# First wave of a one-layer encoder: four adaLN column tiles computed on TensorE, with ten more landing buffers

## Chip, core and metric

The kernel runs on one core of a Trainium2 chip. The metric is device time in microseconds (us) for one execution of the whole program. A core has five engines that run side by side, each with its own instruction queue in program order: TensorE (PE in the profile, with its weight loads shown as PEld), VectorE (DVE), ScalarE (ACT), GpSimd (POOL) and SyncE (SP), which here issues the DMA transfers between HBM and the on-chip memory. Products go to PSUM, which has eight banks of 128 x 512 floats.

## What is computed

One layer of an encoder over 2048 tokens of width 1024, everything in float32. A conditioning vector c gives six vectors of 1024 (shift, scale and gate for each of two sublayers); the first sublayer is windowed attention, the second a SwiGLU network. Cut to the part that matters here:

```python
c_act = silu(c)
mod = c_act @ ada_w + ada_b                    # 1024 -> 6 * 1024
sh1, sc1, g1, sh2, sc2, g2 = split(mod, 6)
h = rmsnorm(x, mix_norm_pre) * (1 + sc1) + sh1
qkv = h @ w_qkv                                # 1024 -> 1536
x = x + g1 * rmsnorm(attention(qkv) @ w_o, mix_norm_post)
h = rmsnorm(x, ffn_norm_pre) * (1 + sc2) + sh2
x = x + g2 * rmsnorm(swiglu(h), ffn_norm_post)
```

So the first product of the layer, `h @ w_qkv`, can start only when the norm of x and the first tiles of sh1 and sc1 exist.

## The kernel before

**Layout.** Activations are held transposed: width on the 128 partitions (KT = 8 tiles k of 128 rows), tokens along the free dimension, in four chunks of CH = 512 tokens. A float32 product is made of three products of a shorter format (`three`, line 839): each operand is split into a high part `hi` and a rest `lo` (`split`, line 845: ScalarE copies to `hi`, a second engine subtracts to get `lo`), and hi\*hi, hi\*lo and lo\*hi are added up in PSUM.

**The first wave** is the part that the change touches (lines 966 to 982). It works on chunk 0 and on seven of the twelve 128-column tiles of w_qkv (WAVE = 7), and keeps seven PSUM banks open while k runs from 0 to 7. Before the loop, `squares0` (line 877) squares the eight x tiles on ScalarE and adds them in pairs on VectorE, and `norm` (line 887, `rstd_of` at line 810) sums over the partitions by a product with a tile of ones (plain float32 operands, which the profile shows as two MATMULs for each product), then takes Ln and Exp on ScalarE and one correction step: Square on ScalarE, three operations on VectorE. Then, for each k:

- two tiles of ada_w, one for the scale and one for the shift (128 x 1024 floats each), are loaded (`ada_load`, line 945) and each is multiplied with silu(c) and summed along its rows by one VectorE instruction (`ada_reduce`, line 950). For this, `cb` holds silu(c) copied to all 128 partitions.
- `coef` = (1 + scale) \* gain, a 128 x 1 operation on VectorE;
- `w_piece(k, 0)` (line 955) loads 896 columns of w_qkv and splits them, the subtraction being recorded for GpSimd;
- `Chunk.h` (line 891): x \* r on VectorE, then scale and shift on ScalarE, then a cast to `hi` on ScalarE, then `lo` on VectorE;
- 21 products of 128 x 512 on TensorE (7 tiles, 3 products each).

After the loop come the rests of the w_qkv columns (`w_piece(k, 1)`, 640 columns, into the pool w2), the five other tiles of chunk 0, then chunk 1 with all twelve tiles, then attention with chunks 2 and 3 as filler, the output projection and the feed-forward part.

**Buffers.** All loads of ada_w and w_qkv land in one pool `raws` with five buffers of 128 x 1024 floats (line 933); pool w2 (line 932) holds the split rests of w_qkv, 40 KB in each partition.

**Order.** The program does not fix the order of instructions. All operations are first recorded (`Recorder`, line 136); a planner (`schedule`, line 683) then simulates them with a cost for each (`cost`, line 246), chooses the order on every engine, the buffer of every tile and, for subtractions recorded for GpSimd, whether GpSimd or VectorE does them (`others`, line 225), and repeats this 18 times with priorities taken from the run before. DMAs are in the same plan, all on SP's queue. So a local edit gives a new plan for the whole program. All instructions are emitted from one line, 748, so the profile is read by tile names: `ada` (tiles of ada_w), `wqkv` (raw weights), `w` (split weights), `x`, `hi`, `lo`, `nsq` (squares), `nr` and `nta` (the norm), `cb`, `mod`, `coef`, and `bank` for PSUM.

Of the kernel before, what the change touches and what calls it, by code (L numbers as in the profile page):

```python
# [20 lines left out]
P = 128  # L21
S = 2048
D = 1024
# [31 lines left out]

OBUFS = 6

HOLD = 6

PARTS = ((2, 3, 3, 3), (3, 3, 3, 2))  # L60
# [24 lines left out]
class Buf:  # L85


    def __init__(self, rec, name, shape, dtype, pool, tag):
        self.name, self.shape, self.dtype, self.pool, self.tag = name, list(shape), dtype, pool, tag
        self.row = int(np.prod(shape[1:]))  # L90
        self.unit = 1 if self.row <= P else DH
        self.log, self.ops, self.slot, self.real = [], set(), None, None


class Tag:
# [40 lines left out]
class Recorder:  # L136
# [41 lines left out]
    def record(self, eng, fn, args, kw):  # L178
        op = Op()
        op.i, op.eng, op.fn, op.args, op.kw, op.ins = len(self.ops), eng, fn, args, kw, None  # L180
        aps = [(j, x) for j, x in list(enumerate(args)) + list(kw.items()) if isinstance(x, bass.AP)]
        out = {0}
        if fn == "custom":
            out = {1}
        elif fn == "tensor_tensor_reduce":
            out = {0, 7}
        elif fn == "activation" and "accum_out" in kw:
            out = {0, "accum_out"}
        op.writes = [self.region(x) for j, x in aps if j in out]
        op.reads = [self.region(x) for j, x in aps if j not in out]  # L190
        op.tiles = []
        if fn == "matmul" and not kw.get("start"):
            op.reads.append(op.writes[0])
        elif fn == "matmul":
            op.writes = [(op.writes[0][0], (3, (1 << P) - 1))]
        outs, ins = [x for j, x in aps if j in out], [x for j, x in aps if j not in out]
        op.forms, op.calls, op.stamp = {}, {}, 0
        for op.eng, op.fn, op.args, op.kw in (*self.others(eng, fn, args, kw, ins), (eng, fn, args, kw)):
            self.cost(op, outs, ins)
            op.forms[op.eng] = op.occ, op.lat, op.port, op.table  # L200
            op.calls[op.eng] = op.fn, op.args, op.kw
        op.eng_first = eng
        op.pred = {}
        for w, items in ((False, op.reads), (True, op.writes)):
            for b, m in items:
                for q, qw, qm in b.log:
                    if (w or qw) and q is not op and qm[0] & m[0] and qm[1] & m[1]:
                        op.pred[q] = max(op.pred.get(q, 0), self.gap(q, op))
        for w, items in ((False, op.reads), (True, op.writes)):
            for b, m in items:  # L210
                if w:
                    b.log = [e for e in b.log if not (e[2][0] | m[0] == m[0] and e[2][1] | m[1] == m[1]) or e[0] is op]
                b.log.append((op, w, m))
                if b.tag is not None and op not in b.ops:
                    if not b.ops:
                        b.tag.order.append(b)
                    b.ops.add(op)
                    op.tiles.append(b)
        op.succ = []
        for q in op.pred:  # L220
            q.succ.append(op)
        self.ops.append(op)
        return op
# [22 lines left out]
    def cost(self, op, outs, ins):  # L246
# [12 lines left out]
        elif eng == "pe":  # L259
            if fn == "transpose":  # L260
                op.occ, op.lat = 108, 330
            elif outs[0].dtype == F32 and ins[0].dtype == F32:
                op.occ, op.lat = 860 * n // CH, 1060 * n // CH
            else:
                op.occ = n * 0.4167 + 13.5
                op.lat = op.occ + 162
# [487 lines left out]
    return ap.bitcast(F32)  # L754


def row(ap, n):

    return bass.AP(tensor=ap.tensor, offset=ap.offset, ap=[[0, P], [1, n]])
# [3 lines left out]
def encoder_layer(ctx, tc, a):  # L763
# [34 lines left out]
    mod = const.tile([P, 80], F32, name="mod")  # L798
    adab = constr.tile([P, 48], F32, name="adab")
    gains = constr.tile([P, 4, KT], F32, name="gains")  # L800
    nsink = const.tile([P, HEADS], F32, name="nsink")
    ones = const.tile([P, P], F32R, name="ones")
    ident = const.tile([P, P], F32, name="ident")
# [52 lines left out]
    class Chunk:  # L856
# [20 lines left out]
        def squares0(self):  # L877

            sq = [hs.tile([P, CH], F32, tag=("hi", "lo")[k % 2], name=f"nsq0_{k}") for k in range(KT)]
            for k in range(KT):  # L880
                act.activation(sq[k], self.xt[k], AF.Square)
                if k % 2:
                    dve.tensor_tensor(sq[k - 1], sq[k - 1], sq[k], ALU.add)
            dve.tensor_tensor(sq[6], sq[4], sq[6], ALU.add)
            self.acc = [sq[0], sq[2], sq[6]]

        def norm(self, psp, ptag):
            r = nrm.tile([P, CH], F32, tag="nr", name=f"nr{self.c}")
            self.r = rstd_of(rot(nrm, "nsq", 2), psp, ptag, self.acc, f"a{self.c}", r)
# [39 lines left out]


    with ExitStack() as pa:
        w2 = open_pool(pa, "w2", side="right")
        raws = open_pool(pa, "raws", 5, side="right")
        w1 = open_pool(pa, "w1", side="right")
        psA = open_pool(pa, "psA", 8, space=PSUM)

        cb = nrm.tile([P, D], F32, name="cb")
        sp.dma_start(cb, row(a["c"], D))
        ch0 = Chunk(0)
        sp.dma_start(adab, a["ada_b"])  # L940
        sp.dma_start(gains, a["gains"])
        act.activation(cb, cb, AF.Silu)
        sp.dma_start(cb_d, cb)

# [5 lines left out]
        def ada_reduce(t, w):  # L950
            dve.tensor_tensor_reduce(w, w, cb, 1.0, adab[:, t:t + 1], ALU.mult, ALU.add, mod[:, t:t + 1])

        wres = {}

        def w_piece(k, i):
            pl, lo_c, n = ((w1, 0, C1), (w2, C1, C2))[i]
# [24 lines left out]
        for k in range(KT):  # L981
# [847 lines left out]
```

## Time and profile before

| what | value |
|---|---|
| median of three runs | 2037.0 us (2036.87 to 2037.06) |
| the profiled execution's own time | 2036.67 us |
| span of its instructions | 2034.9 us |
| mean granted TensorE clock | 0.995 of full speed |
| TensorE busy | 1991.0 us (98%) |
| VectorE busy | 1703.6 us (84%) |
| ScalarE busy | 1069.9 us (53%) |
| GpSimd busy | 554.4 us (27%) |
| HBM traffic | 278.52 MB read, 134.77 MB written |

In the lines of the profile, a timeline row gives the start, the length, the engine, the source line, the operation, `out<-in`, the shape and how many were merged into the row; in brackets stands how long the engine had been idle before and what released it. A row of the windows view gives, for a stretch of time, the busy time of each engine and its number of instructions, the granted clock (PEclk), the busy share of the DMA engines and their rate. A group row ends with the busy time in us and the mean of one in ns. Matmuls are pipelined: a row of eight that lasts 1.98 us holds eight that start 0.227 us apart.

### The profile page before, as it was taken

How to read it: one execution, taken by the hardware profiler on the slowest of the kernel's cores; microseconds unless marked ns; L12 is line 12 of the kernel's file. 1: busy time of each engine (PE TensorE's matmuls, PEld its weight loads, DVE VectorE, ACT ScalarE, POOL GpSimd, SP SyncE). 2: the span in 40 equal slices, each digit the busy share in tenths (PEclk: the TensorE clock that was granted, in tenths of full speed). 3: DMA queues.
4: the chain of work that ended last, by engine and by line, in shares of the span. 5: the costliest groups of instructions: out<-in, count | busy, mean ns of one | idle time of the engine just before them, and what ended most of it. 6: DMA issues, size and time to landing. Idle time of an engine off the chain costs nothing.

```text
span 2034.9 us, 28945 instructions
## 1 busy us (share of the span) xinstructions
PE 1991.0 (98%) x9366; PEld 1659.3 (82%) x9366; DVE 1703.6 (84%) x3075; ACT 1069.9 (53%) x2094; POOL 554.4 (27%) x501
## 2 busy tenths in 40 slices
PE   5999999999999999999999999999999999999997
PEld 4888888888787778788888888888888888888886
DVE  7868888877989888988787998776776789989998
ACT  5557766777778864344343533333333744455432
POOL 1302342344657513432333221111111000120031
PEclk9999999999999999999999999999999999999999
DMA  8896765576787694444446743333233694398543
GB/s 308 303 324 211 241 210 173 192 279 229 253 279 251 226 361 150 160 161 166 165 160 242 272 155 130 119 135 104 83 124 105 240 334 144 117 326 297 173 154 109
DMA packets 208580, 415.23 MB, mean 204 GB/s; under 512 B 19963, under 2 KB 61996, under 8 KB 205356
## 3 DMA queue, kind: packets, MB, share of 16 engines
q1 hardware_dynamic: 207852, 412.84, 58.7%
q8 instruction: 75, 1.23, 0.2%
q14 instruction: 77, 0.63, 0.1%
q10 hardware_dynamic: 576, 0.52, 0.1%
HBM read 278.52 MB, written 134.77 MB: 203 GB/s over the span
## 4 chain that ended last, share of the span: by engine, by line
PE 91%; DVE 5%; DMA 2%; issue 1%; ACT 1%; SPq 0%; POOL 0%; DVEq 0%; ACTq 0%; POOLq 0%
PE bank L748 91%; DVE z L748 1%; DVE ada L748 1%; DVE zx L748 1%; DVE pr L748 0%; DMA o_d<-of 0%; DMA ly<-y_d 0%; DMA x<-xT 0%; DMA ol<-o_d 0%; SPq L748 0%; DVE u_i L748 0%; DMA ada<-ada_w 0%; DVE x L748 0%; DVE plo L748 0%; DVE ws_i L748 0%
## 5 line engine op out<-in xcount | busy, mean ns | idle before, releaser
L748 PE MATMUL bank<-ht,ws_i 128*128 128x512 f32 x1584 | 374.0, 389 | 0.0
L748 PEld LDWEIGHTS bank<-ht,ws_i 128*128 128x128 f32 x1584 | 297.3, 188 | 61.7
L748 PE MATMUL bank<-hb,wa_i 128*128 128x512 f32 x1056 | 254.2, 389 | 0.4 <-DVE hb L748 0.4
L748 PEld LDWEIGHTS bank<-hb,wa_i 128*128 128x128 f32 x1056 | 198.1, 188 | 42.0 <-DVE hb L748 0.7
L748 PE MATMUL bank<-ol,wo 128*128 128x512 f32 x768 | 206.1, 396 | 2.3 <-ACT yacc L748 1.1
L748 DVE TENSOR_TENSOR u_i<-bank,u_i 128x512 f32<-128x512 f32 x176 | 120.9, 688 | 80.0 <-PE bank L748 77.8
L748 ACT CAST ws_i<-s_i 128x512 fp32r<-128x512 f32 x132 | 81.9, 620 | 192.2 <-DVE s_i L748 96.2
L748 ACT ACTIVATE pr<-pr,nm 128x385 f32<-128x385 f32 (+1 forms) x256 | 154.8, 606 | 53.3 <-DVE nm L748 47.4
L748 DVE CUSTOM_DVE_ANT_0 pr<-bank,bias,nsink 128x384 f32<-128x384 f32 (+1 forms) x256 | 149.9, 594 | 25.6 <-PE bank L748 22.0
L748 PEld LDWEIGHTS bank<-ol,wo 128*128 128x128 f32 x768 | 141.2, 188 | 28.7 <-ACT yacc L748 1.5
L748 POOL TENSOR_SCALAR pr<-pr,rs 128x384 f32<-128x384 f32 (+1 forms) x177 | 114.7, 660 | 179.7 <-DVE rs L748 168.3
L748 POOL TENSOR_TENSOR p_i<-p_i,u_i 128x512 f32<-128x512 f32 x41 | 66.9, 1632 | 344.6 <-DVE u_i L748 173.9
L748 POOL TENSOR_TENSOR z<-z,z 128x512 f32<-128x512 f32 x29 | 45.4, 1577 | 345.9 <-ACT ws_o L748 264.4
L748 PE MATMUL bank<-k,q 128*128 128x384 f32 (+1 forms) x512 | 135.5, 345 | 1.5 <-DVE nm L748 1.5
L748 PE MATMUL bank<-hi,ws 128*128 128x512 f32 x384 | 134.3, 400 | 0.0
L748 DVE TENSOR_TENSOR plo<-bank,phi 128x512 fp32r<-128x512 f32 x184 | 120.8, 684 | 9.8 <-ACT phi L748 8.7
L748 PE MATMUL bank<-hb,ws_i 128*128 128x512 f32 x528 | 127.1, 390 | 1.8 <-ACT p_i L748 1.8
L748 ACT CAST wa_i<-wiri 128x512 fp32r<-128x512 f32 x132 | 81.3, 620 | 90.1 <-PE bank L748 78.4
L748 PE MATMUL bank<-ht,wa_i 128*128 128x512 f32 x528 | 126.8, 389 | 0.0
L748 DVE TENSOR_TENSOR wa_i<-wiri,wa_i 128x512 fp32r<-128x512 f32 x132 | 103.4, 784 | 19.0 <-ACT wa_i L748 19.0
L748 PEld LDWEIGHTS bank<-hb,ws_i 128*128 128x128 f32 x528 | 98.9, 188 | 23.2 <-ACT p_i L748 2.6
L748 DVE TENSOR_TENSOR z<-bank,z 128x512 f32<-128x512 f32 (+1 forms) x164 | 107.7, 659 | 11.4 <-PE bank L748 10.2
(261 smaller groups left out, 4422.6 us busy)
## 6 DMA issues: line engine op xcount, KB each, us to landing
wiri<-w_in SPq DMA_DIRECT2D x88, 512.0 KB, 4.6
ada<-ada_w SPq DMA_DIRECT2D x40, 512.0 KB, 5.1
q_d<-e SPq DMA_DIRECT2D x32, 512.0 KB, 4.4
q<-q_d SPq DMA_DIRECT2D x16, 1024.0 KB, 7.0
wo<-wo_d SPq DMA_DIRECT2D x16, 1024.0 KB, 6.0
wiro<-w_out SPq DMA_DIRECT2D x40, 384.0 KB, 5.0
g_d_b<-p_i SPq DMA_DIRECT2D x44, 256.0 KB, 3.3
g_d_t<-p_i SPq DMA_DIRECT2D x40, 256.0 KB, 2.0
```

Source lines behind the costliest of these rows:

```text
L748: o.ins = getattr(engs[o.eng], o.fn)(*args, **kw)
```

## The change

- For k = 0 and 1 (`ADA_PE = 2`), the two ada_w tiles are loaded from a second copy laid out the other way (`ada_t`, prepared on the host), and each becomes eight products of one column on TensorE with plain float32 operands, weights 128 x 128, moving operand one column of silu(c); a 128 x 1 addition on VectorE adds the bias. silu(c) in columns (`ct`, 128 x 8) is a new small load and a new small Silu. For k = 2 to 7 the VectorE reduction stays.
- Tiles of ada_w land in a new pool `raws0` with ten buffers, which takes the place of w2; w2 is opened when `raws0` is closed after the loop. The raw w_qkv pieces keep the five buffers of `raws`.
- The subtraction in the split of the first 896 columns is recorded for VectorE alone; that of the other 640 columns stays with GpSimd.
- The norm of chunk 0 loses one VectorE addition (four sums go to TensorE in place of three), and its correction step becomes three VectorE operations without the Square on ScalarE.
- For chunk 0, `hi` is written by the scale and shift itself; a second one writes x for `lo`.
- Fourteen products of the tile of ones with itself (128 columns, float32), whose result nobody reads, are recorded ahead of the squares.
- The planner's cost for a float32 product gets a lower bound (230 ns), and its record keeps the one-column products into one bank apart by column.

```diff
+ADA_PE = 2
+WARM = 14
...
-    def rstd_of(alloc, psp, ptag, acc, tag, r=None, direct=False):
+    def rstd_of(alloc, psp, ptag, acc, tag, r=None, direct=False, short=False):
...
         act.activation(r, ps, AF.Ln, bias=epsc)
         act.activation(r, r, AF.Exp, scale=-0.5)
+        if short:
+            dve.scalar_tensor_tensor(t, ps, EPS, r, ALU.add, ALU.mult)
+            dve.scalar_tensor_tensor(t, t, -0.5, r, ALU.mult, ALU.mult)
+            dve.scalar_tensor_tensor(r, t, 1.5, r, ALU.add, ALU.mult)
+            return r
         act.activation(t, r, AF.Square)
...
-            dve.tensor_tensor(sq[6], sq[4], sq[6], ALU.add)
-            self.acc = [sq[0], sq[2], sq[6]]
+            self.acc = sq[::2]
...
-            act.activation(xt, xt, AF.Identity, bias=mod[:, k:k + 1], scale=coef[:, 0, k:k + 1])
             self.hh[k] = (hi, lo)
+            if c == 0:
+                act.activation(hi, xt, AF.Identity, bias=mod[:, k:k + 1], scale=coef[:, 0, k:k + 1])
+            act.activation(xt, xt, AF.Identity, bias=mod[:, k:k + 1], scale=coef[:, 0, k:k + 1])
+            if c == 0:
+                return scaled, dve.tensor_tensor(lo, xt, f(hi), ALU.subtract)
             return scaled, split(hi, lo, xt, dve)
...
-        w2 = open_pool(pa, "w2", side="right")
         raws = open_pool(pa, "raws", 5, side="right")
         w1 = open_pool(pa, "w1", side="right")
+        first = ExitStack()
+        raws0 = open_pool(first, "raws0", KT * C2 * 2 // D, side="right")
...
+        sp.dma_start(ct, a["ct"])
         sp.dma_start(cb, row(a["c"], D))
...
+        act.activation(ct, ct, AF.Silu)
         act.activation(cb, cb, AF.Silu)
...
+        ada_ps = psA.tile([P, CH], F32, tag="mm", name="ada_ps")
+        columns(nc, ada_ps)
+
+        def ada_products(k):
+
+            for e, t in enumerate((8 + k, k)):
+                w = raws0.tile([P, D], F32, tag="raw", name=f"adat{t}")
+                sp.dma_start(w, a["ada_t"][t])
+                j = 2 * k + e
+                for i in range(KT):
+                    pe.matmul(ada_ps[:, j:j + 1], w[:, i * P:(i + 1) * P], ct[:, i:i + 1],
+                              start=i == 0, stop=i == KT - 1)
+                dve.tensor_tensor(mod[:, t:t + 1], ada_ps[:, j:j + 1], adab[:, t:t + 1], ALU.add)
...
-            split(t[:, 0], t[:, 1], w[:, :n], pool)
+            split(t[:, 0], t[:, 1], w[:, :n], pool if i else dve)
...
+        warm = psA.tile([P, CH], F32, tag="mm", name="warm")
+        for _ in range(WARM):
+            pe.matmul(warm[:, :P], f(ones), f(ones), start=True, stop=True)
         ch0.squares0()
...
         for k in range(KT):
-            ada_reduce(*ada_load(8 + k, raws))
-            ada_reduce(*ada_load(k, raws))
+            if k < ADA_PE:
+                ada_products(k)
+            else:
+                ada_reduce(*ada_load(8 + k, raws0))
+                ada_reduce(*ada_load(k, raws0))
...
+        first.close()
+        w2 = open_pool(pa, "w2", side="right")
```

More of the change, by code (lines that the diff above doesn't have):

```diff
@@ L92, in __init__ @@
         self.log, self.ops, self.slot, self.real = [], set(), None, None
+        self.group = None
 class Tag:
@@ L193, in record @@
             op.reads.append(op.writes[0])
-        elif fn == "matmul":
+        elif fn == "matmul" and op.writes[0][0].group is None:
             op.writes = [(op.writes[0][0], (3, (1 << P) - 1))]
@@ L218, in record @@
                     op.tiles.append(b)
+        if eng == "pe" and op.writes[0][0].group is not None:
+            for q in op.writes[0][0].group:
+                op.pred.setdefault(q, 0)
+            op.writes[0][0].group = [op]
         op.succ = []
@@ L754, in f, with columns @@
     return ap.bitcast(F32)
+def columns(nc, ap):
+    b = nc.bufs[ap.tensor.name]
+    b.unit, b.group = 1, []
 def row(ap, n):
@@ L800, in encoder_layer @@
     gains = constr.tile([P, 4, KT], F32, name="gains")
+    ct = constr.tile([P, KT], F32, name="ct")
     nsink = const.tile([P, HEADS], F32, name="nsink")
@@ L883, in squares0 @@
                     dve.tensor_tensor(sq[k - 1], sq[k - 1], sq[k], ALU.add)
-            dve.tensor_tensor(sq[6], sq[4], sq[6], ALU.add)
-            self.acc = [sq[0], sq[2], sq[6]]
+            self.acc = sq[::2]
         def norm(self, psp, ptag):
             r = nrm.tile([P, CH], F32, tag="nr", name=f"nr{self.c}")
-            self.r = rstd_of(rot(nrm, "nsq", 2), psp, ptag, self.acc, f"a{self.c}", r)
+            self.r = rstd_of(rot(nrm, "nsq", 2), psp, ptag, self.acc, f"a{self.c}", r,
+                             short=self.c == 0)
         def h(self, k):
@@ L1806 @@
         "ada_w": np.asarray(ada_w)[0].T.reshape(6 * KT, P, D),
+        "ada_t": np.asarray(ada_w)[0].reshape(KT, P, 6 * KT, P)[:, :, :KT + ADA_PE].transpose(2, 1, 0, 3)
+        .reshape(KT + ADA_PE, P, D),
+        "ct": np.asarray(c).reshape(KT, P).T,
         "ada_b": cols(ada_b[0]),
```

4 lines of the change are left out of this document (2 added, 2 removed).

## The prediction

> **What bounds the kernel now.** I read the windows view first, to see in which stretch TensorE is not full.
>
> ```profile
> span 2034.9 us, 28945 instructions
> 0.00:20.00 20.00, 6.20 (x6) 1.50 (x6) 8.80 (x15) 12.66 (x16) 0.70 (x6) 1.00 0.90 320
> 20.00:40.00 20.00, 16.30 (x61) 13.22 (x62) 18.61 (x32) 10.37 (x14) 2.92 (x1) 1.00 0.89 309
> 40.00:60.00 20.00, 16.78 (x63) 13.29 (x61) 19.96 (x27) 10.35 (x15) 8.99 (x4) 0.83 0.86 279
> 60.00:540.00 480.00, 479.06 (x2544) 411.28 (x2543) 389.12 (x901) 336.26 (x744) 167.68 (x203) 1.00 0.70 240
> 540.00:720.00 180.00, 172.21 (x879) 141.23 (x878) 157.75 (x361) 143.85 (x317) 106.52 (x115) 0.99 0.77 258
> 720.00:2000.00 1280.00, 1278.21 (x5653) 1057.56 (x5652) 1077.71 (x1668) 548.17 (x970) 267.63 (x174) 1.00 0.51 180
> ```
>
> After the span's length, the first pair behind each stretch is TensorE. From 60 to 540 and from 720 to 2000 us it is busy 99.8% of the time, so what is won before 60 us is kept unless something later breaks the flow. Before 60 it is not full. TensorE's timeline shows how:
>
> ```profile
> 23.70 3.35 PE L748 MATMUL bank<-hi,w 128*128 128x512 f32 x7 [8.09 <-ACT hi L748]
> 26.85 0.63 PE L748 MATMUL bank<-lo,w 128*128 128x512 f32 x1
> ...
> 28.56 0.58 PE L748 MATMUL bank<-lo,w 128*128 128x512 f32 x1
> 28.97 0.39 PE L748 MATMUL bank<-hi,w 128*128 128x512 f32 x1
> ...
> 45.08 1.98 PE L748 MATMUL bank<-hi,w 128*128 128x512 f32 x8
> 50.28 0.79 PE L748 MATMUL bank<-lo,w 128*128 128x512 f32 x1 [3.22 <-DVE lo L748]
> ...
> 55.99 2.13 PE L748 MATMUL bank<-hi,w 128*128 128x512 f32 x8
> 57.96 0.39 PE L748 MATMUL bank<-lo,w 128*128 128x512 f32 x1
> ```
>
> Dense products start (1.98 - 0.39) / 7 = 0.227 us apart (row at 45.08). So the wave's 8 x 21 products are 38.1 us of work. Four losses stand in these rows:
> - the first product starts at 23.70;
> - the first twelve (seven, and five from 26.85 to 28.56) take 28.97 - 23.70 = 5.27 us instead of 2.72: a slow start of 2.5;
> - the row at 45.08 should be followed at 46.9 and is followed at 50.28: a hole of 3.4, ended by VectorE's `lo`;
> - 21 products (thirteen, then eight) take 57.96 - 50.28 = 7.68 instead of 4.77: a second slow start, 2.9.
>
> The last three make 8.8 us. Check by count: 61 + 63 products at 0.227 are 28.1 of the 40 us from 20 to 60; 11.9 are lost, and 3.7 + 8.8 is 12.5 with the edges. The first is the way to 23.70, from the timeline of the other engines:
>
> ```profile
> 8.76 3.21 ACT L748 ACTIVATE nsq<-x 128x512 f32<-128x512 f32 x5 [2.82 <-DMA x<-xT]
> 11.99 1.28 ACT L748 ACT_TABLE_LOAD   x1
> 12.01 1.42 DVE L748 TENSOR_TENSOR nsq<-nsq,nsq 128x512 f32<-128x512 f32 x2 [0.63 <-ACT nsq L748]
> 13.28 1.06 ACT L748 ACTIVATE cb<-cb 128x1024 f32<-128x1024 f32 x1
> 13.57 2.04 PE L748 MATMUL bank<-nsq,ones 128*128 128x512 f32 x2 [1.32 <-DVE nsq L748]
> 14.36 1.28 ACT L742 ACT_TABLE_LOAD   x1
> 15.65 0.69 ACT L748 ACTIVATE nr<-bank,epsc 128x512 f32<-128x512 f32 x1
> 17.13 0.62 ACT L748 ACTIVATE nr<-nr 128x512 f32<-128x512 f32 x1
> 18.45 0.69 DVE L748 SCALAR_TENSOR_TENSOR nta<-bank,nta 128x512 f32<-128x512 f32 x1
> 19.06 1.27 DVE L748 CUSTOM_DVE_ANT_0 ada<-ada,cb,adab 128x1024 f32<-128x1024 f32 x1
> 20.72 0.69 DVE L748 TENSOR_TENSOR nr<-nr,nta 128x512 f32<-128x512 f32 x1
> 21.44 0.69 DVE L748 TENSOR_TENSOR x<-x,nr 128x512 f32<-128x512 f32 x1
> 22.19 0.81 ACT L748 ACTIVATE x<-x,mod,coef 128x512 f32<-128x512 f32 x1
> ```
>
> ScalarE's chain (table, Silu of `cb`, table) and the last product of the squares both end at 15.6, then come Ln, Exp and the correction, in which an adaLN reduction (19.06) stands in the way on VectorE.
>
> **The change, part by part.**
>
> *Way to the first product.* The last square still ends at 11.97, for x lands no sooner. One addition goes: the sum is ready at 12.70, the first of the two in the row at 12.01. If TensorE is fast by then, that product takes 1.03 instead of 2.04 (the row at 101.14 below) and ends at 13.75. If the planner puts both Silus into ScalarE's idle time before 8.76, Ln starts there; if they stay, at 15.65 plus a small Silu. So Ln starts at 13.75 to 15.75. Then Ln and Exp 1.36 with the hand-over, three dependent VectorE operations of about 0.65, x 0.65, `hi` 0.86: 4.8, and 0.9 more if a weight cast slips in between Ln and Exp (before, Exp starts at 17.13, 0.8 after Ln's end). That gives 18.6 to 21.5; I take 19.9: **3.8 gained**.
>
> *Column products.* No row shows a one-column product. The nearest:
>
> ```profile
> 74.06 0.52 PE L748 MATMUL bank<-w,hi 128*128 128x256 f32 x3
> 74.42 0.28 PE L748 MATMUL bank<-w,lo 128*128 128x256 f32 x1
> 101.14 1.03 PE L748 MATMUL bank<-oh,rb 33*16 33x511 f32 x2
> L748 PEld LDWEIGHTS bank<-ht,ws_i 128*128 128x128 f32 x1584 | 297.3, 188 | 61.7
> ```
>
> Products of 256 columns, each with its own weight load, start (74.42 - 74.06) / 3 = 0.12 apart, so a load fits into 0.12. A float32 product is two MATMULs (rows at 13.57 and 101.14). No row sets a floor, so the lower bound is 0; the upper is two loads and two products end to end, 2 x (0.19 + 0.28) = 0.94. I take 2 x 0.12 = 0.24, the row with one load for each product: sixteen for one k are 3.8 us. The data: x is 2.1 MB, `cb` and k = 0's two tiles 1.6 MB, at the first window's 320 GB/s, start-up included, here at 11.6; with 2 us in hand I take 14. k = 0's products then run from 14 to 17.8, ahead of 19, when `coef` is wanted: hidden. k = 1's end at 21.6, 1.7 after the first product could start: **2 lost** (0 to 3.8).
>
> *The hole and VectorE.* What makes VectorE late at 50 us:
>
> ```profile
> 46.42 3.19 DVE L748 CUSTOM_DVE_ANT_0 ada<-ada,cb,adab 128x1024 f32<-128x1024 f32 x1
> 46.44 2.08 POOL L748 TENSOR_TENSOR w<-wqkv,w 128x896 fp32r<-128x896 f32 x1 [21.15 <-DMA ada<-ada_w]
> L748 DVE CUSTOM_DVE_ANT_0 ada<-ada,cb,adab 128x1024 f32<-128x1024 f32 x16 | 24.0, 1512 | 0.9 <-ACT cb L748 0.9
> L748 DVE TENSOR_TENSOR w<-wqkv,w 128x896 fp32r<-128x896 f32 x4 | 4.3, 1087 | 1.7 <-ACT w L748 1.7
> ```
>
> The reduction beside GpSimd's subtraction takes 3.19 instead of 1.27: VectorE waits it out. The four subtractions that move to VectorE cost 4 x 1.0; four reductions less save 4 x 1.2, and the stalls, (1.512 - 1.27) x 16 = 3.9 on reductions alone, mostly go. For k of 2 to 7 VectorE then needs 2 x 1.2 + 1.0 + 2 x 0.6 + 0.1 = 4.7 for each k, TensorE 21 x 0.227 = 4.77. k = 2's tiles land at about 6.7 MB / 320 GB/s = 21; by 22 VectorE also has k = 0 and 1 behind it (two times 1.0 + 1.2, beside the norm, from 13 on) and ends at 22 + 6 x 4.7 = 50; TensorE wants k = 7 at 19.9 + 1.7 + 7 x 4.77 = 55. Five us of slack, less what GpSimd's 640-column splits stall if they start before 50. So **3.4 gained**, 1 given back (0 to 3.4).
>
> *Landing places.* Before, a load waits for a buffer:
>
> ```profile
> 15.70 0.33 SPq L748 DMA_DIRECT2D wqkv<-w_qkv  x1
> 21.34 0.94 ACT L748 CAST w<-wqkv 128x896 fp32r<-128x896 f32 x1 [2.93 <-DMA wqkv<-w_qkv]
> ```
>
> The second weight piece is issued at 15.70, when the first reduction frees its tile, and keeps ScalarE waiting to 21.34. With fifteen buffers it is issued with the rest. The wave needs 2.1 + 0.5 + 8 x 1.5 = 14.7 MB; at the windows' 279 to 320 GB/s the last piece lands at 46 to 53. k = 7 is wanted at 55, so this holds with a wide margin at the upper rate and just so at the lower; the risk is in the 1 us above. w2's space is free only after the reductions of k = 5 to 7, about 41 to 50, and TensorE has work of its first wave until 19.9 + 1.7 + 38.1 = 60: no new hole. Behind a w2 split that waits for its space stand, on ScalarE, the casts after it, and on GpSimd nothing before 60. The second scale-and-shift costs ScalarE 0.81 where the cast cost 0.62, and ScalarE is about half idle (10.4 of 20 us). The small DMA for `ct` ahead of `cb` costs SP one issue and is hidden behind x.
>
> *Slow starts.* Fourteen warming products of 128 columns, each a quarter of the slow 2.04 at 13.57, end by 8 us; the first squares' sum waits a little, the last doesn't. Both slow starts come after 8.1 and 3.2 us of idle TensorE (the brackets at 23.70 and 50.28); the granted clock of the third window, 0.83, holds the second. Early warming alone wouldn't reach 19.9, but the squares' products (three groups up to 13.75) and the column products (14 to 21.6) leave no idle stretch of 3 us. **2.5 and 2.9 gained.** The Trainium skill (TensorE: Matmul & The Clock Gate, "Part 1: The HAM clock gate") has the clock fall to half after an idle window of about 3.4 us and come back after as long under load. By that rule products at 1 us do nothing for one at 20, and if the column products don't hold the clock, they run at half of it themselves. The trace agrees on the fall (3.2 idle sufficed); the return took 5.3 and about 6 us here.
>
> *Sum.* 3.8 + 2.5 + 3.4 + 2.9 - 2 - 1 = 9.6 off the profiled execution's 2036.67: 2027.1; the median shown is 0.3 higher. I say **2027** (own range 2024 to 2030).
>
> **The rivals.**
> - *Everything hides* (0.15): Ln at 13.75, first product at 18.6, column products out of the way, no hole: 5.1 + 8.8 = 13.9, **2023**. For: VectorE's and DMA's slack. Against: it needs the planner to find all of it.
> - *The clock isn't held* (0.14): k = 0's products run at 0.48 until the clock is back after the 5.3 us of the first slow start: eleven of them, then five at 0.24, end at 20.5, and the first `hi` comes at 21.6, 1.7 later; k = 1's 3.8 then lie wholly in the way, 1.8 more: 3.5 less gained, **2031**. For: 3.2 us of idling was enough once. Against: no such stretch in my schedule.
> - *Given back later* (0.14): DMA.
>
> ```profile
> 70.00:80.00 10.00, 10.00 (x76) 9.56 (x75) 8.30 (x13) 4.05 (x7) 2.58 (x2) 1.00 1.00 370
> ```
>
> Just after the wave the DMA engines are full. Chunk 1 and w2 wanted 10 us sooner would need 60 to 100 us at a rate that this row already has, and the plan is new everywhere: the 7.8 us that TensorE idles from 540 to 720 could grow. Then 2 us or less remain: **2035**.
> - *Slower: column products are dear* (0.10). The place is k = 0 and 1 on TensorE, in order ahead of the wave. With c for one, both sets end at 14 + 32 c; against 19.9 the wave loses 32 c - 5.9, and this decides where it eats the 11.6 gained elsewhere: from c = 0.55 on. At the bound of 0.94 it is 24.2 - 11.6 = 12.6 slower: **2049**. Against: the 0.12 spacing.
>
> **How the numbers follow.** The forecast has 0.47. What a measurement can tell from no change is about 0.2%, 4 us. Faster by more: 0.47 + 0.15 + 0.14 = 0.76; within 0.2%: "given back", 0.13 of its 0.14; slower: 0.10 and the rest, 0.11. The range, 2022 to 2036, holds the first three and most of "given back"; it leaves out the slow case and some tails, 0.18.
>
> **What would show it.** Right: the first 128x512 product of `hi` and `w` near 20 us with starts 0.23 apart; column products two MATMULs each, 0.1 to 0.15 apart; no reduction of 3 us in the wave; `lo` ending no TensorE idle time before 60; about 40 us for the first 165 products from then on. Wrong: column products over 0.25 apart, starts at 0.43 after 20 us, a hole before `w2` is split, or more idle time after 60 us than now.

## The result, and the profile after

The changed kernel takes 2067.72 us (median of four runs, 2067.05 to 2068.58), beside 2037.03 us (2036.87 to 2037.91) for the kernel before: a ratio of 1.0153, 95% interval 1.0141 to 1.0165. It is 30.7 us slower, where 10 us faster was forecast and 2036 was the end of the range. The profiled execution took 2067.43 us with a span of 2065.6.

The windows view of the kernel after, by the stretches that the prediction used (TensorE busy, its weight loads, VectorE, ScalarE, GpSimd, granted clock, DMA share, GB/s):

```profile
0.00:20.00 20.00, 15.81 (x74) 11.93 (x74) 4.41 (x10) 10.04 (x14) 0.70 (x6) 0.85 0.89 327
20.00:40.00 20.00, 19.75 (x78) 16.87 (x78) 14.78 (x28) 10.89 (x13) 0.00 (x0) 0.72 1.02 404
40.00:60.00 20.00, 20.00 (x88) 16.05 (x86) 18.50 (x30) 11.91 (x17) 2.66 (x1) 1.00 0.54 165
60.00:540.00 480.00, 477.44 (x2508) 405.72 (x2507) 379.15 (x896) 334.31 (x739) 174.95 (x201) 1.00 0.70 239
540.00:720.00 180.00, 171.01 (x872) 138.17 (x870) 164.30 (x367) 142.15 (x316) 105.80 (x115) 1.00 0.74 249
720.00:2000.00 1280.00, 1278.98 (x5532) 1039.45 (x5533) 1055.41 (x1637) 545.36 (x961) 263.26 (x174) 1.00 0.52 180
```

The last row holds the surprise. From 720 to 2000 us TensorE is as busy as before (1278.98 of 1280 us, before 1278.21) and its clock is full, but it gets through 5532 products where it got through 5653: 2.1% fewer in the same time. TensorE does not wait; each product takes longer. TensorE's timeline in the feed-forward part of the kernel after shows which ones:

```profile
1651.90 2.20 PE L756 MATMUL bank<-ht2o,ws_o 128*128 128x512 f32 x9
1653.94 2.26 PE L756 MATMUL bank<-hb21o,wa_o 128*128 128x512 f32 x9
1656.04 2.26 PE L756 MATMUL bank<-ht3o,ws_o 128*128 128x512 f32 x9
```

and in the kernel before:

```profile
1652.27 2.20 PE L748 MATMUL bank<-ht4o,wa_o 128*128 128x512 f32 x9
1654.31 2.20 PE L748 MATMUL bank<-hb22o,ws_o 128*128 128x512 f32 x9
1656.35 4.02 PE L748 MATMUL bank<-hb11o,wa_o 128*128 128x512 f32 x17
```

Read the starts: before, nine products take 1654.31 - 1652.27 = 2.04 us, 0.2267 each. After, the nine of `ht2o` still do (1653.94 - 1651.90), but the nine of `hb21o` take 2.10, 0.2333 each: 3% more. The groups by tile agree (kernel after, then before; the number behind the comma is the mean of one in ns, 7 ns more for `hb21o`):

```profile
L756 PE MATMUL bank<-hb21o,wa_o 128*128 128x512 f32 x240 | 59.9, 396 | 0.0
L756 PE MATMUL bank<-ht2o,ws_o 128*128 128x512 f32 x240 | 58.1, 389 | 0.0
```

```profile
L748 PE MATMUL bank<-hb21o,wa_o 128*128 128x512 f32 x240 | 58.3, 389 | 0.0
L748 PE MATMUL bank<-ht2o,ws_o 128*128 128x512 f32 x240 | 58.1, 389 | 0.0
```

`ht2o` and `hb11o` lie in a pool on the left side of the on-chip memory (low addresses), as the weights of this part do; `hb21o` and the four others lie in a pool on the right. Pairs on one side kept their pace (`hb11o` to 0.6%: 0.228), pairs on different sides lost 3%. What moved is one side against the other: `ct`, 32 bytes in each partition, was added to the constants on the right (`constr`), so that every right-hand pool behind it starts 32 bytes lower. Before, both sides' pools start at multiples of 512 bytes (2560 on the left, 228864 on the right: the kernel's two ends, 1152 and 229344, and the sizes of the constants).

The first half of the feed-forward part shows that it is the distance that counts, and not either address. There the blocks of seven steps take their weights from a left and a right pool in turn (`wi[i % len(wi)]`). Kernel after:

```profile
929.53 2.96 PE L756 MATMUL bank<-hb,ws_i 128*128 128x512 f32 x12
932.33 2.96 PE L756 MATMUL bank<-hb,wa_i 128*128 128x512 f32 x12
...
949.09 2.89 PE L756 MATMUL bank<-hb,ws_i 128*128 128x512 f32 x12
951.82 2.91 PE L756 MATMUL bank<-hb,wa_i 128*128 128x512 f32 x12
```

The `ws_i` rows are the same step of two blocks, with a moving tile on the right. With weights on the left its twelve products take 932.33 - 929.53 = 2.80 us; with weights on the right, where both operands are 32 bytes off their old place, 951.82 - 949.09 = 2.73, the old pace (twelve times 0.2267 are 2.72).

The first wave is the second place that differs. TensorE, VectorE and ScalarE in the timeline of the kernel after:

```profile
1.05 4.75 PE L756 MATMUL bank<-ones 128*128 128x128 f32 x28 [1.05 <-DVE rb L756]
...
9.68 4.83 PE L756 MATMUL bank<-nsq,ones 128*128 128x512 f32 x6 [2.27 <-DVE nsq L756]
...
14.34 2.07 PE L756 MATMUL bank<-ct,adat 128*128 128x1 f32 x18
...
16.45 0.16 DVE L756 TENSOR_TENSOR mod<-bank,adab 128x1 f32<-128x1 f32 x1 [4.23 <-PE bank L756]
...
16.66 3.62 PE L756 MATMUL bank<-ct,adat 128*128 128x1 f32 x20 [0.25 <-DVE mod L756]
17.24 0.69 DVE L756 SCALAR_TENSOR_TENSOR nta<-nta,nr 128x512 f32<-128x512 f32 x1
20.31 0.16 DVE L756 TENSOR_TENSOR mod<-bank,adab 128x1 f32<-128x1 f32 x1 [2.38 <-PE bank L756]
20.39 0.68 DVE L756 SCALAR_TENSOR_TENSOR nr<-nta,nr 128x512 f32<-128x512 f32 x1
...
20.53 5.28 PE L756 MATMUL bank<-ct,adat 128*128 128x1 f32 x24 [0.25 <-DVE mod L756]
...
21.83 0.81 ACT L756 ACTIVATE hi<-x,mod,coef 128x512 fp32r<-128x512 f32 x1 [4.97 <-DVE x L756]
...
25.66 3.33 PE L756 MATMUL bank<-hi,w 128*128 128x512 f32 x7
```

The first product of the wave starts at 25.66, later than before (23.70), though `hi` is there at 22.6: TensorE works on column products until then, and its next seven are slow (3.33 us where seven dense ones take 1.75). The column MATMULs start 0.11 us apart at first and 0.21 apart from 17.6 us on: the eighteen of the first row take 2.07 us, the twenty-four of the third 5.28. And on VectorE the small additions of `mod` wait in order for them: the norm's last step, ready after 17.9, runs at 20.39 behind one that waited 2.38 us.

### The profile page after: what moved, and what is told of

Its sections match the earlier page's. It is cut to its first block, busy times and chain, and to the rows that moved or that the text cites. A ratio compares the mean times of both kernels' runs of the same rounds, so it can differ in the third digit from the quotient of the medians.

```text
span 2065.6 us, 29099 instructions
## 1 busy us (share of the span) xinstructions
PE 2035.0 (99%) x9460; PEld 1674.0 (81%) x9460; DVE 1689.5 (82%) x3070; ACT 1073.2 (52%) x2095; POOL 554.5 (27%) x501
## 4 chain that ended last, share of the span: by engine, by line
PE 91%; DVE 4%; DMA 2%; ACT 1%; issue 1%; POOL 0%; SPq 0%; DVEq 0%; ACTq 0%; POOLq 0%
PE bank L756 91%; DVE pr L756 1%; DVE z L756 1%; DVE zx L756 0%; DVE plo L756 0%; DVE ada L756 0%; DMA ada<-ada_w 0%; DMA ol<-o_d 0%; DMA hd_d_t<-hf 0%; DVE x L756 0%; DMA x<-xT 0%; DMA xr<-xT 0%; ACT pr L756 0%; DVE lo L756 0%; DMA hf<-h_d 0%
## 5 line engine op out<-in xcount | busy, mean ns | idle before, releaser
L756 PE MATMUL bank<-ht,ws_i 128*128 128x512 f32 x1584 | 378.3, 392 | 0.0
L756 PE MATMUL bank<-hb,wa_i 128*128 128x512 f32 x1056 | 258.4, 393 | 0.0
L756 PE MATMUL bank<-ol,wo 128*128 128x512 f32 x768 | 210.6, 402 | 4.8 <-DVE ol L756 1.9
L756 POOL TENSOR_TENSOR p_i<-p_i,u_i 128x512 f32<-128x512 f32 x38 | 61.7, 1624 | 363.5 <-DVE u_i L756 199.2
L756 POOL TENSOR_TENSOR z<-z,z 128x512 f32<-128x512 f32 x32 | 50.5, 1589 | 340.9 <-ACT ws_o L756 263.7
L756 PEld LDWEIGHTS bank<-ht,wa_i 128*128 128x128 f32 x528 | 99.2, 188 | 23.1
```

Source lines behind the costliest of these rows:

```text
L756: o.ins = getattr(engs[o.eng], o.fn)(*args, **kw)
```

## The experiments

To see where time is won or lost within a run, I compare the start of the same product in two kernels, and name it by the TensorE work ahead of it: its products at the dense spacings of the trace of before (512 columns 0.2267 us, 384 0.175, 256 0.12, 128 0.109; about 1960 us in all). This gives the table to which the points below refer: us ahead of the kernel before, in the profiled executions.

```
work ahead of it (us)       100    600    700   1000    end
after                       0.8   -2.3   -9.6  -12.3  -29.9
before_pad_right            0.4   -4.3   -5.0   -9.0  -26.6
ct_inner                    1.0    1.8   -5.6   -3.2   -4.2
columns_only               -0.9   -2.9   -8.8   -6.8   -6.8
ct_inner_no_columns         4.8    7.5   -0.1    2.3    1.2
warm_only                   4.0    6.3   -0.4    1.8    0.5
nc_hold                     5.9    6.9    0.2    2.6    1.3
nc_spare600                 5.4   10.0    2.7    4.1    1.4
nc_spare1000                8.1    6.9   -1.0    1.4    0.2
nc_hold_spare1000           8.7    6.5    2.5    4.9    3.9
nc_late22                   4.5    5.9   -1.6    0.2   -1.0
nc_late44                  -0.8    1.7   -5.1   -2.9   -4.3
before_late22               0.5    0.6   -0.7   -0.6   -0.7
```

("end" is the last product. The products that only some kernels have, the warming, column, holding and repeated ones, are not counted as work.)

### The address, or a state that the column products leave?

My theory was that the distance in bytes between the sides sets the pace; the first rival, that the new products leave TensorE slower.

**before_pad_right**: the kernel before and nothing else than 32 unused bytes; every instruction stands in its old place.

```diff
     coef = constr.tile([P, 4, KT], F32, name="coef")
+    constr.tile([P, KT], F32, name="pad_right")
```

> The kernel before with one unused 32-byte tile in the same pool and nothing else; order of instructions unchanged. Theory A: 0.231 to 0.235 us between starts for pairs from two sides, 2037 + 28 = 2065 (2058 to 2072). Theory S: 2037.

Measured: 2062.21 us, ratio 1.0125 (1.011 to 1.014). Its window from 720 on:

```profile
720.00:2000.00 1280.00, 1278.86 (x5536) 1039.42 (x5536) 1057.62 (x1644) 542.35 (x961) 258.41 (x168) 1.00 0.52 180
```

5536 products, as in the kernel after. Thirty-two bytes that nobody reads cost 25.5 us by the ratio (22 to 29); the table shows the loss growing with the work, 17.6 us from 1000 to the end.

**after_no_columns**: the kernel after with `ADA_PE = 0` and `WARM = 0`, `ct` left where it is.

> The changed kernel without one-column products (all adaLN tiles by VectorE reductions) and without warming products; ct stays where it is. Theory A: dense starts still 0.231 to 0.235 for pairs from two sides, 2060 to 2068. Theory S: back at 0.227, 2030 to 2040. The first wave starts earlier than 25.7 us if the one-column products were what held it.

Measured: 2065.78 us, ratio 1.0141 (1.0126 to 1.0156). Without any column or warming product it is as slow: the rival falls.

**after_pad_right** and **after_pad_left**: the kernel after with 32 more bytes on the right, or with 32 on the left.

```diff
     coef = constr.tile([P, 4, KT], F32, name="coef")
+    constr.tile([P, KT], F32, name="pad_right")
```

```diff
     ones = const.tile([P, P], F32R, name="ones")
+    const.tile([P, KT], F32, name="pad_left")
```

> The changed kernel with one more unused 32-byte tile in the pool that holds ct, so that all right-hand pools move down by another 32 bytes (64 in all); order of instructions unchanged. In the trace after, dense products of 512 columns start 0.231 to 0.235 us apart over the whole kernel where the weights lie in a left-hand pool and the moving tile in a right-hand one, or the other way round, and 0.227 where both lie on one side. Theory A (address): ct's 32 bytes moved the right-hand pools against the left-hand ones by half of 64 bytes, and that costs 28 us over the kernel: starts back at 0.227 everywhere, time 2067.7 - 28 = 2039 (2034 to 2042). Theory S (state): the one-column or the warming products leave TensorE slower for good: 2067 as before.

> The changed kernel with one more unused 32-byte tile in the left-hand constants instead, so that left-hand pools too are 32 bytes off a multiple of 64. Theory A in its relative form (what counts is that weights and moving tile lie in the same half of 64 bytes): starts 0.227, time 2039 (2034 to 2042), like the pad on the right. Theory A in its absolute form (a tile off 64 bytes is slow by itself): all pairs slow, slower than 2067, about 2085. Theory S: 2067.

Measured: 2066.69 us, ratio 1.0146 (1.0131 to 1.0161), and 2067.39 us, ratio 1.0152 (1.0135 to 1.0169). I had held 64 bytes for the period; that was a miss. A distance of 64 is as slow as one of 32, from either side. In after_pad_left all left-hand pools are 32 bytes off as well, and `ht2o`, with its weights on its own side, keeps its mean of 389 ns: once more the distance, and not the address.

**before_pad_128, before_pad_512, before_pad_256**, one execution each: the edit of before_pad_right with 128, 512 and 256 bytes.

> The kernel before with 128 unused bytes in the right-hand constants, same order of instructions. In the kernel before, left-hand and right-hand tiles all start at multiples of 512 bytes. Theory A with a period of 128 bytes or less: 2036. With a longer period: 2062 as with 32.

> The same with 512 unused bytes. Theory A with a period that divides 512: 2036, starts at 0.227. Rival: any further tile in that pool, or anything but the distance of addresses, makes it slow: 2062.

> The kernel before with 256 unused bytes in front of the right-hand pools; with 128 it took about 24 us more and with 512 none. If the period is 256: 2036.5 and dense starts of 0.227; if it is 512: about 2060 and dense starts of 0.231 to 0.235 where weights and moving tile lie on different sides.

Measured: 2060.31, 2036.54 and 2036.18 us. The window from 720 on with 128 bytes:

```profile
720.00:2000.00 1280.00, 1278.73 (x5546) 1040.65 (x5545) 1058.55 (x1647) 541.87 (x959) 258.66 (x169) 1.00 0.52 180
```

and with 256:

```profile
720.00:2000.00 1280.00, 1278.24 (x5654) 1058.14 (x5653) 1076.20 (x1668) 549.27 (x971) 265.08 (x174) 1.00 0.51 179
```

Distances of 32, 64 and 128 are slow, 0, 256 and 512 are fast: of the sizes tried, the multiples of 256 bytes.

**ct_inner**: the kernel after, with `ct` in a pool of its own inside the stack that is closed after the wave. The order of instructions is that of the kernel after.

```diff
-    ct = constr.tile([P, KT], F32, name="ct")
...
         raws0 = open_pool(first, "raws0", KT * C2 * 2 // D, side="right")
+        ct = open_pool(first, "ctp", side="right").tile([P, KT], F32, name="ct")
```

> The changed kernel with ct in a pool of its own inside the first wave's stack, so that no other pool moves; order of instructions the same as in the changed kernel, ct's place and the right-hand addresses alone differ. The runs so far: 32 unused bytes alone cost the kernel before 26.3 us (2035.9 to 2062.2), and a shift of 64 bytes on one side is as slow as one of 32. Theory A (the distance between left-hand and right-hand addresses sets the pace of dense products; zero, as before the change, is the fast one): starts at 0.227, time 2066 - 26 = 2040 (2036 to 2044). Rival P (the changed plan itself is slow): over 2055.

Measured: 2042.26 us, ratio 1.0027 (1.0017 to 1.0037), and from 720 on:

```profile
720.00:2000.00 1280.00, 1279.35 (x5643) 1057.98 (x5643) 1077.25 (x1660) 552.36 (x974) 271.21 (x179) 1.00 0.52 180
```

The same instructions, 25.5 us faster. So of the 30.7 us some 25 are the address and 6 are left for the change itself.

### What the column products do

**ct_inner_no_columns**: ct_inner with `ADA_PE = 0`, `WARM = 0`. What stays of the change: the landing places, the splits on VectorE, the short norm, `hi` written directly.

> As ct_inner, without one-column and warming products (all adaLN tiles by VectorE reductions). At one and the same address distance, TensorE's position shows this plan 3.4 us ahead of the kernel before at 80 us and some 2 us behind at the end, because of idle time at 700 to 725 us. Theory A: 2036 + 2 = 2038 (2033 to 2042), first dense product near 20.6 us, 5 us ahead of ct_inner. If the one-column products cost nothing on TensorE: no earlier than ct_inner.

Measured: 2035.62 us, ratio 0.9994 (0.9985 to 1.0003). That is 6.7 us less than ct_inner. At 100 us of work 3.8 us of it are there (4.8 ahead against 1.0); the rest comes later, in a plan that differs everywhere, so 6.7 is the price of the columns with their plan. Its first product starts at 21.31.

**columns_only** and **warm_only**: ct_inner with the columns but `WARM = 0`, and with the warming products but `ADA_PE = 0`.

> As ct_inner, with the one-column products kept and no warming products. Theory C: one-column products at 0.11 or 0.22 apart by the clock, not holding it; k = 1's set ahead of the wave, so that it starts at 25 us or later, and slowly; total 2038 to 2046. If the one-column products are not what costs: first product near 21 us.

> As ct_inner, with the fourteen warming products kept and no one-column products. Theory C: no gain from warming at 1 us, the wave starts near 21 us and slowly (0.43 for 1 to 5 us). If warming is worth what I forecast, starts 0.227 apart from the first product on. Total 2030 to 2040 with the new plan.

Measured: 2043.41 us, ratio 1.003 (1.0017 to 1.0044), and 2037.44 us, ratio 1.0004 (0.9995 to 1.0014). The version with columns is as slow without the warming products. Warm_only's TensorE:

```profile
1.05 5.98 PE L756 MATMUL bank<-ones 128*128 128x128 f32 x28 [1.05 <-DVE rb L756]
6.87 1.02 PE L756 MATMUL bank<-nsq,ones 128*128 128x512 f32 x2
...
11.59 1.12 PE L756 MATMUL bank<-nsq,ones 128*128 128x512 f32 x2 [0.18 <-DVE nsq L756]
20.60 3.24 PE L756 MATMUL bank<-hi,w 128*128 128x512 f32 x7 [7.88 <-ACT hi L756]
```

The warming products do make the squares' products fast (1.02 where before had 2.04), but after 7.88 us of idling the seven take 3.24 us again.

**nc_hold**: ct_inner_no_columns, with seven 512-column products of the same kind as the squares' behind the norm, where TensorE idled.

```diff
         ch0.norm(psA, "mm")
+        hold = psA.tile([P, CH], F32, tag="mm", name="hold")
+        for _ in range(7):
+            pe.matmul(hold, f(ones), ch0.acc[-1], start=True, stop=True)
         steps = []
```

> As ct_inner_no_columns, with seven plain float32 products of 512 columns recorded behind the last product of the norm, whose result nobody reads, so that TensorE has work from about 13 us to the first wave. Theory C (TensorE's clock falls in the idle time ahead of the wave, and only products close to it, with many columns, hold it): first products 0.227 apart at once, 1.5 to 2.5 us won at 40 us against ct_inner_no_columns at the same first product. Rival: first products at 0.43 all the same. The total also carries a new plan, 2030 to 2040.

Measured: 2036.28 us, ratio 1.0 (0.9991 to 1.001). TensorE:

```profile
8.57 11.64 PE L756 MATMUL bank<-nsq,ones 128*128 128x512 f32 x20 [0.56 <-DVE nsq L756]
20.23 1.88 PE L756 MATMUL bank<-hi,w 128*128 128x512 f32 x7
```

Seven in 1.88 us: the wave starts at full pace. The granted clock is 1.00 from 16 to 24 us, where ct_inner_no_columns has 0.57 (16 to 20) and 0.50 (20 to 24). So the idle stretch did cause the slow start, and 512-column products hold the clock where one-column products don't. At 100 us of work it is 1.1 us ahead of the version without; at the end nothing of this is left.

### Where the rest of the gain goes

Without columns every version with `ct` moved leads by 4 to 9 us at 100 us of work, and every one loses 4 to 8 us between 600 and 700, at the end of attention. Is it another engine's limit, or the order of work?

**nc_spare600**: ct_inner_no_columns with another of the planner's constants (`SPARE`, 800 to 600), which lays the same work in another order.

> As ct_inner_no_columns, with one constant of the planner changed (the margin that it adds to every DMA, 800 to 600 ns): the same operations in another order, everywhere in the program. Theory L (what the plan loses between 640 and 730 us, some 5 us more than the kernel before, is the luck of one plan): the loss there moves by 2 us or more either way, total 2029 to 2041. Rival E (an earlier first wave must wait there for something at a fixed time): the loss stays within 1 us, total 2035 to 2036.

Measured: 2036.99 us, ratio 1.0009 (0.9997 to 1.002): 10.0 us ahead at 600, 2.7 at 700.

**nc_late22** and **nc_late44**: the first product of the wave issued 22 or 44 more times, put in while the finished plan is written out, so that no order changes.

```diff
+                if o.eng == "pe" and not late and o.args[0].tensor.name.startswith("psq0_"):
+                    late.append(o)
+                    for _ in range(22):
+                        nc.tensor.matmul(*args, **{**kw, "stop": True})
                 if o.fn == "custom":
```

> The version without columns, with the first 512-column product of the wave issued 22 more times in front of itself (same operands, each starting its bank anew), put in after the order of work is fixed: every other instruction stands where it stood. 22 x 0.227 = 5.0 us later from the first wave on, so it is at about 0 against the kernel before at 100 us of work, where the version without was 4.8 ahead. Theory E (something other than TensorE ends last at 640 to 720 us and eats what was won): the end moves by 0 to 1.5 us, 2035.6 to 2037.1. Theory P (the time is lost there because this kernel's plan is worse there, and TensorE's time before it carries through): the end moves by 5, 2040.6.

> The same with 44 products in front, 10 us later. Theory E: the 7.5 us by which the version without was ahead at 600 us of work are used up, and only what goes beyond shows: 2.5 to 4 us, 2038 to 2039.6. Theory P: 10 us, 2045.6.

Measured: 2037.17 us, ratio 1.0006 (0.9998 to 1.0015), and 2041.34 us, ratio 1.0028 (1.0018 to 1.0039). The window from 640 to 720 us of the kernel before, and then of ct_inner_no_columns, nc_late22 and nc_late44:

```profile
640.00:720.00 80.00, 75.48 (x381) 60.92 (x380) 70.11 (x149) 66.83 (x139) 44.20 (x47) 1.00 0.75 253
```

```profile
640.00:720.00 80.00, 73.08 (x350) 57.17 (x349) 70.55 (x146) 62.32 (x130) 37.07 (x41) 0.96 0.69 241
```

```profile
640.00:720.00 80.00, 73.34 (x350) 57.38 (x349) 70.97 (x148) 63.34 (x133) 38.43 (x43) 0.96 0.70 243
```

```profile
640.00:720.00 80.00, 73.23 (x362) 57.96 (x360) 73.08 (x158) 62.11 (x133) 39.91 (x45) 0.98 0.71 249
```

TensorE idles 6.7 to 6.9 us here whether its work comes at its time or later, where the kernel before idles 4.5, and its clock is 0.96 to 0.98 here, before 1.00. The expectations for both took each 5 us of products for 5 us of delay, which was wrong: those of nc_late22 filled part of the slow start and the short waits for the splits of w2 (0.68, 0.22 and 1.37 us between 59 and 66 us), and it is only 0.3 us behind the version without at 100 us of work and 1.6 at the end, which decides nothing. nc_late44 is 5.6 behind at 100, 5.0 at 700, and ends 5.7 us later. By theory E the 7.5 us of lead at 600 would have swallowed that: theory E falls, and what TensorE loses early arrives at the end.

By elimination that leaves the order of work. Part of the loss is a chain that moves along, here in ct_inner_no_columns:

```profile
701.43 0.42 SPq L756 DMA_DIRECT2D ol<-o_d  x1
707.15 1.04 ACT L756 CAST ol<-ol 128x1024 fp32r<-128x1024 f32 x1 [4.34 <-DMA ol<-o_d]
```

```profile
708.25 0.72 PE L756 MATMUL bank<-ol,wo 128*128 128x512 f32 x2 [2.19 <-ACT ol L756]
710.54 6.85 PE L756 MATMUL bank<-ol,wo 128*128 128x512 f32 x16 [1.56 <-DVE ol L756]
```

The last attention output is read back, split, and TensorE waits for each step; behind the waits its clock is low (0.68 from 710 to 720 us), and sixteen products take 6.85 us where dense ones take 3.8. In nc_late22 the read is issued at 702.83 instead of 701.43, in nc_late44 at 706.97, and the two waits of nc_late22 are 1.72 and 2.02. The kernel before has the same chain, with the read issued at 703.13 and split from 710.30 on, so that the read is not slower now (5.7 us from issue to split, before 7.2); but other products lie in between, the waits are shorter, and the clock stays at 1.00:

```profile
711.40 0.73 PE L748 MATMUL bank<-ol,wo 128*128 128x512 f32 x2 [0.73 <-ACT ol L748]
712.66 2.55 PE L748 MATMUL bank<-ol,wo 128*128 128x512 f32 x10 [0.53 <-DVE ol L748]
```

The chain is about half of what ct_inner_no_columns loses: from 650 to 660 us of work its lead falls from 3.4 to -0.2. The other 4 us go between 600 and 650, and what takes them was not traced.

**before_late22**: the 22 products in the kernel before.

> The same 22 products in front of the wave of the kernel before, every other instruction in its place. If the hole at 46.9 to 50.28 is VectorE's alone, and the second slow start comes only of the hole, as the prediction has it, 5.0 us later closes both: at 100 us of work +5.0 - 3.4 - 2.9 = about -1.3. If the second slow start comes of something else, +1.6. The end by theory E: within 1.5 of 2036.7 either way; by theory P it moves as the place at 100 us does.

Measured: 2036.55 us, ratio 1.0001 (0.9992 to 1.001). Its third window, which had 16.78 us of TensorE in the kernel before:

```profile
40.00:60.00 20.00, 20.00 (x90) 16.58 (x89) 19.96 (x27) 10.45 (x15) 8.97 (x4) 1.00 0.85 289
```

Five us of useless products cost nothing: the hole and the second slow start are gone, and at 100 us of work 5.0 paid bought 5.5. I had expected it 1.3 ahead there if the two were one thing, and 1.6 behind if not; it is 0.5 ahead. So the second slow start came of the hole.

**nc_spare1000** and **nc_hold_spare1000**: ct_inner_no_columns and nc_hold with `SPARE` at 1000.

> The version without columns with the planner's SPARE at 1000 instead of 800: the same work, laid in another order. Theory P (what is given back after 540 us belongs to the order of work of one plan): TensorE's loss between 540 and 860 us may come out anywhere between the 18.9 us of the kernel before and 22.4, and the end with it, 2031.5 to 2036; if it stays 21 to 22.4 in this plan as in the four others of this wave, every plan that follows this wave has it, and the cause is the wave, not one order.

> The same with the seven products behind the norm, which gave a dense first wave: about 1 us earlier at 100 us of work than without them. Theory P: as in the run beside it, and 1 us earlier, 2030.5 to 2036; under 2032.0 it would beat both kernels by what can be measured.

Measured: 2036.65 us, ratio 1.0008 (0.9999 to 1.0016), and 2034.37 us, ratio 0.999 (0.9981 to 0.9999). From 100 to 700 us of work the six orders of this wave give back 2.7 to 9.1 us; none gives back nothing. The size of it differs from order to order. The last version ends furthest ahead, and its interval is the only one on the fast side that leaves out 1. It is 2 us ahead (0.2 to 3.9), half of the 4 us that the prediction took as the least that can be told, and it is one of six orders, so it shows no gain for certain. Why each of them is worse there than the order before isn't settled: no run keeps the order after 540 us and changes the wave alone.

## Why the prediction was wrong

- **The step that failed first** is "what is won before 60 us is kept": it, and the sum, took the 0.227 us of a dense product as the kernel's constant. No term and no rival had a pace that changes. `ct` was costed as one issue, hidden; its 32 bytes cost 25 of the 30.7 us. The 1940 us in the three windows after 60 us, where the prediction looked for idle time only, were where each percent of pace is worth 19 us. This was not the only step that was enough by itself: with `ct` moved, the kernel still takes 2042.26 us, 6 us slower where 10 faster was forecast, and those 6 go with the column products.
- **Column products.** Their price at full clock was right (0.12 a MATMUL forecast, 0.11 measured). What failed is "leave no idle stretch of 3 us": that was true, and didn't help, for the clock stood at half all the same, here and, behind an idle stretch of 2.27 us, from 11 to 14 us too (0.50). The windows of the kernel after, from 14 to 26 us:

```profile
14.00:18.00 4.00, 3.75 (x29) 3.32 (x28) 1.45 (x3) 2.25 (x3) 0.00 (x0) 0.93 1.04 405
18.00:22.00 4.00, 3.75 (x18) 3.67 (x19) 1.69 (x5) 0.17 (x1) 0.00 (x0) 0.50 1.02 411
22.00:26.00 4.00, 4.00 (x19) 4.00 (x20) 0.96 (x3) 3.94 (x5) 0.00 (x0) 0.50 1.03 406
```

  TensorE is busy for 3.75 to 4.00 of each 4 us, and the clock falls to 0.50. The rival "the clock isn't held" is what this part did; with the 2 us already forecast for k = 1 it came to 5.5, and the version with columns was 6.7 slower. It put k = 0's and k = 1's products in the wave's way, rightly, and left out VectorE, where the additions for the columns hold up the norm. The Trainium skill (TensorE: Matmul & The Clock Gate, "Part 1: The HAM clock gate") has the gate follow how busy TensorE is and give full speed after some 3.4 us of sustained work; the trace does not agree for work of this kind: the clock fell to half some 3 us into 11 us of column products, and did not come back under them.
- **Way to the first product.** Forecast 19.9, bounds 18.6 to 21.5; without columns it starts at 20.2 to 21.3: right, for the kernel without that part.
- **The hole and the second slow start.** Gone, and the second slow start came of the hole: right. The first slow start stayed in all versions but those with seven wide products behind the norm (in the two delayed ones and before_late22 the repeated products took it). In the kernel before, the granted clock on record is 1.00 all through it (20 to 40 us), so that a low clock as its cause is read from the other versions.
- **VectorE and the landing places.** All twelve reductions of the wave take 1.28 us, and no wait for raw weights shows on TensorE: right. The 1 us set aside was spent on short waits for w2.
- **The sum at 100 us of work** was 9.6 ahead; the kernel after with `ct` moved has 1.0, without columns 4.8, with wide products 5.9, and with these and another order 8.7. So for a kernel that holds the clock otherwise the terms were 1 to 4 us too high in sum, by the order.
- **"Given back later"** happened to every version without columns, in the stretch that the rival named (540 to 720) and at about its price (2035 forecast, 2035.6 measured), but not by its mechanism, so that the agreement in size is luck. It gave the DMA engines right after the wave as the cause, and there is no loss there: from 60 to 540 us ct_inner_no_columns has TensorE busy for 477.46 of 480 us, and its lead grows from 4.8 at 100 us of work to 7.5 at 600. The loss comes at the end of attention and is put down to the order of work by elimination.

## What to carry to other kernels

Before adding a tile to a pool that stays open, see what it does to the addresses of all that lies behind it: put small tiles where they shift nothing, or fill up to a multiple of 256 bytes, which was fast here, and compare the number of products in a long dense window, not only the busy share. Work that is meant to hold TensorE's clock has to be close to where it is needed and of wide products (512 columns did it here, one column did not). And a gain early in a planned program is worth what the new plan keeps of it: check it at several places down the run, and with a delay that changes no order.

## What the runs showed of the hardware that was not expected

- The pace of dense 512-column products with a weight load each depends on the distance between the addresses of weights and moving tile: 0.2267 us with the sides 0, 256 and 512 bytes off the first layout, 0.233 (means by tile from 0.2327 to 0.2335) at 32, 64 and 128, for five of the seven output tiles; the two on the weights' side have 0.2267 and 0.228. Both operands moved by 32 bytes together are at the old pace (2.73 us for twelve). The Trainium skill (SBUF — State Buffer, "Who interferes with whom") gives TensorE two read ports, independent of each other, and has it wait on nobody; here the same instructions cost 25 us more with one operand shifted by 32 bytes, so the measurement decides. Which part of the memory makes it was not tried.
- One-column float32 MATMULs with a weight load each start 0.11 us apart at first and 0.21 apart when the clock has fallen to 0.50, and a busy stretch of them does not keep the clock up (0.50 from 18 to 26 us).
